# Mixture-of-experts trunk: the small experts' values turned in two pieces at other places of the gate-up, and up to three down blocks a step in the last pair of experts

## The chip, the cores and the metric

The kernel runs on one core of one Trainium2 chip. The metric is the device time of one execution in microseconds (us). TensorE is called PE in the profile, its weight loads PEld, VectorE DVE, ScalarE ACT, GpSimd POOL, SyncE SP; SP issues the weight loads by DMA.

## The reference, cut to what matters

The program is a decoder trunk of two layers over 256 tokens of 1024 channels, in fp32. The change touches the second layer's expert part alone, the last large stage before a gated embedding add and the final norm:

```python
def moe_swiglu(hn, w_router, w_gate_up, w_down):
    xt = hn.reshape(T, D)                       # 256 x 1024
    logits = (xt @ w_router).astype(jnp.float32)
    top_val, top_idx = lax.top_k(logits, TOP_K) # 2 of 8 experts
    gates = jax.nn.softmax(top_val, axis=-1)
    ...
    def expert_block(args):
        xb, e = args
        g, u = jnp.split(xb @ w_gate_up[e], 2, axis=-1)   # 1024 -> 2 x 3584
        return (jax.nn.silu(g) * u) @ w_down[e]           # 3584 -> 1024
    ...
    contrib = y[dest] * g_s[:, None].astype(y.dtype)
    out = jnp.zeros((T, D), y.dtype).at[tok_s].add(contrib)
```

All expert weights, 8 x (1024 x 7168 + 3584 x 1024) fp32 values, are read once.

## The kernel before

**Products in parts.** An fp32 matrix is split into two parts of the type fp32r: ACT casts the high part `h` (line 145), DVE subtracts it from the raw value and leaves the low part `l` (line 146). A raw weight tile is 1 MB (128 partitions x 2 x 1024); `wsplit` makes two halves of it, each with one cast and one subtraction. There are ten raw buffers and four buffers each for `h` and `l`. DMA fills a raw buffer as soon as its last reader has given it back.

**Two sizes of experts.** The experts are sorted by their number of tokens and taken in the order 0, 4, 1, 5, 2, 6, 3, 7. Experts 0 to 3 ("large") have 128 slots for tokens and need three products for each pair of tiles: h x h, l x h, h x l. Experts 4 to 7 ("small", `few(e)` in the code) have 64 slots; the high and low parts of their tokens stand side by side in the 128 columns, so two products do, and the two halves of the result have to be added.

**Steps.** The hidden width 3584 is cut in chunks of 1024, 1024, 1024 and 512 columns. One step makes the gate and up values of one chunk (`gate_up`): eight channel tiles k, in each 1 MB of gate and up weights; a large expert has 96 products of 512 columns there, a small one 64. 32 steps cover 8 experts; the step's chunk is `now`. Behind the gate-up the step multiplies "down" blocks (`back`, `down`) that belong to chunks finished earlier, usually of the expert before: a block is 512 hidden columns, 2 MB of weights (`r_d`, parts `h_d`, `l_d`), 24 products into `y` for a large expert, 16 for a small one. Before step 8 (RAMP) there is one block a step, from then on two. So a full step from step 8 on has 8 + 4 MB of weights and 16 + 8 halves. After the last down block of an expert, `combine` splits y (`yh`, `yl`, lines 197 and 198), multiplies by the slots (`cb`) and adds to `h` (DVE, line 1260).

**From values to the left operand of down.** A chunk's values must be transposed. For a large expert silu and product come first (`msg`), then `across` transposes a block on PE (`mt<-cst,msg`, line 1226), and `h_T` splits it (`mhh` on ACT, `mhl` on DVE). For a small expert the gate and up values are copied (`msg`, `msu`); in the next step `turn` multiplies each piece of 512 columns by `both`, a matrix that transposes and adds the two halves at once (`mt<-both,msg`, 16 instructions of 64 columns a piece), then `turned` applies silu (ACT, line 1215) and the product (DVE, line 1216) to give `mgu`, and `h_T` splits it (`mh`).

**What sets the order.** A scheduler orders the instructions of each engine by the place at which the code issues them, and moves one ahead where it is ready; `after(...)` pins an instruction behind a named earlier one. Each engine then runs its instructions in order. `gate_up` calls a hook ahead of certain channel tiles; the four hooks of a step, at the tiles of MIDS = (1, 3, 4, 6), counted from 0, are: `turn_fresh` (all pieces of the last chunk), `fresh_turned`, `blocks_across`, `blocks_split`. `turn` has no pin, `turned` and `blocks_split` stand behind the last split issued so far. The hooks run when the split of their tile has been issued.

**The end.** The last pair is experts 3 and 7. Steps 28, 29 and 30 make 7's full chunks with two blocks of expert 3 each, step 31 makes 7's last chunk with the last block of 3. Then come 7's own blocks, two a step, and last the block (7, 3), loaded by halves of the columns (`r_dl`, `l_dl`), each half combined and normed at once.

Of the kernel before, what the change touches and what calls it, by code (L numbers as in the profile page):

```python
# [11 lines left out]
AF = mybir.ActivationFunctionType  # L12
ALU = mybir.AluOpType
AX = mybir.AxisListType
MUL, ADD, SUB, MAX = ALU.mult, ALU.add, ALU.subtract, ALU.max

P = 128
# [66 lines left out]
def trunk_kernel(  # L84
# [6 lines left out]
    pe, act, dve, pool, sync = nc.tensor, nc.scalar, nc.vector, nc.gpsimd, nc.sync  # L91
# [8 lines left out]
    def pa(name, shape=(P, 512)):  # L100
        return ps.tile(list(shape), F32, tag="a", name=name, bufs=4)

    def s2(name, shape, dt=F32):
        return ar.tile(list(shape), dt, tag="s2", name=name, bufs=S2_BUFS)
# [4 lines left out]
    def pt(name, shape=(P, 512)):  # L109
        return ps.tile(list(shape), F32, tag="t", name=name, bufs=2)  # L110
# [62 lines left out]
    def mm(o, a, b, start, stop, shared=False):  # L173
        last["mm"] = pe.matmul(o, a, b, start=start, stop=stop, skip_group_check=shared)  # L174
# [28 lines left out]
    def sub2(pr, *idx):  # L203
        return pr[0][idx], pr[1][idx]
# [17 lines left out]
    BLOCKS = [(b, n) for b in range(NB) for n in range(2)]  # L222
# [21 lines left out]
    def transpose_h(gname, k):  # L244

        q = (pt, py)[k // 4](f"nt_{gname}_{k}", (P, 2, T))
        for b in range(NB):
            for j in range(2):
                pe.transpose(q[:, j, b * P : (b + 1) * P], h[:, b, (k + j) * P : (k + j + 1) * P], ident)
        return q  # L250
# [112 lines left out]
    def ple_proj(i, pT, mark=""):  # L363


        raw = wraw(tview(ple_w_proj[i], 0, 2 * P, 0, D), (2, D), f"pj{i}{mark}")
        if i == 0:
            wt = wsplit(raw, f"pj{i}{mark}")
            wt = {(k, n): sub2(wt[k], slice(None), HALF[n]) for k in range(2) for n in range(2)}
        else:  # L370

            wt = {}
            for k in range(2):
                for n in range(2):
                    wt[k, n] = (s2(f"pwh{i}{k}{n}{mark}", [P, 512], F32R), s2(f"pwl{i}{k}{n}{mark}", [P, 512], F32R))
                    with (ExitStack() if mark else after("yh", "yl")):
                        split(wt[k, n], raw[:, k, HALF[n]])
        banks, res = {}, [[None, None] for b in range(NB)]

        def product(b, n, bank=pa):  # L380
            q = banks[b, n] = bank(f"pj{i}_{b}{n}{mark}")
            for k in range(2):
                mm3(q, sub2(pT, slice(None), k, slice(b * P, b * P + P)), wt[k, n], k == 0, k == 1)

        def copy(b, n):
            res[b][n] = s2(f"pj{i}{b}{n}{mark}", [P, 512])
            act.copy(res[b][n], banks[b, n])

        return product, copy, res
# [553 lines left out]
    def layer1_moe(pT):  # L943
# [3 lines left out]
        product, copy, pj1 = ple_proj(1, pT)  # L947
# [7 lines left out]
        for k in range(0, KT, 2):  # L955
            q = transpose_h("ffn1", k)
# [97 lines left out]
        def few(e):  # L1054
            return e >= FEW
# [115 lines left out]
        def gate_up(e, c, at):  # L1171

            ns = CHUNKS[c][1] // 512
            banks = [[pa(f"m{nm}{e}{c}{i}") for i in range(ns)] for nm in "gu"]
            for k, j, wt in gate_up_weights(e, c):
                if j == 0 and k in at:
                    at[k]()
                products(e, [(banks[j][i], tokens[e][k], sub2(wt, slice(None), slice(i * 512, i * 512 + 512))) for i in range(ns)],
                         k == 0, k == KT - 1)

            def activate():

                res = []
                with after("wcopy", "wsplit"):
                    for i in range(ns):
                        if few(e):
                            res.append([s2(f"ms{nm}{e}{c}{i}", [P, 512]) for nm in "gu"])
                            for j in range(2):
                                act.copy(res[i][j], banks[j][i])
                            continue  # L1190
                        sg = s2(f"msg{e}{c}{i}", [P, 512])
                        act.activation(sg, banks[0][i], AF.Silu)
                        dve.tensor_tensor(sg, banks[1][i], sg, MUL)
                        res.append(sg)
                return res

            return activate

        def turn(e, c):


            res = []
            for i, sg in enumerate(hidden[e, c]):
                q = pt(f"mt{e}{c}{i}", (P, 2, 4, P // 2))
                for j in range(2):
                    for g in range(2):
                        for k in range(2):
                            mm(q[:, j, 2 * g + k, :], sg[j][:, 256 * g + k : 256 * g + 256 : 2], both, True, True)
                res.append(q)
            return res  # L1210

        def turned(e, c, banks):
            t = s2(f"mgu{e}{c}", [P, len(banks), 4, P // 2])
            for i, q in enumerate(banks):
                act.activation(t[:, i], q[:, 0], AF.Silu)
                dve.tensor_tensor(t[:, i], q[:, 1], t[:, i], MUL)
            hidden[e, c] = t

        def across(e, c, i):

# [41 lines left out]
        yb, hT, hidden = {}, {}, {}  # L1262
        both = sm("both", (P, P // 2))
# [87 lines left out]

        gates_up = [(e, c) for e in ORDER for c in range(len(CHUNKS))]
        downs = [(e, c, n) for e in ORDER for c in range(len(CHUNKS)) for n in range(CHUNKS[c][1] // 512)]
        stored = dr.tile([P, NB, 2, 512], F32, name="pj1d")
        fresh = None
        while gates_up or len(downs) > 1:
            now = gates_up.pop(0) if gates_up else None
            step = NE * len(CHUNKS) - len(gates_up) - 1 if now else None
            n = next((i for i, d in enumerate(downs) if d[:2] not in hidden), len(downs))
            n = min(1 if now and step < RAMP else 2, n, sum(d[0] == downs[0][0] for d in downs))  # L1360
            blocks, downs = downs[:n], downs[n:]
            if step == QUAD:
                spread_slots = gather(2)
            if step == SLOTS:
                spread_slots()
            if step == PAIR:
                gather(1)
            banks = {}

            def turn_fresh():  # L1370
                if fresh and few(fresh[0]):
                    banks["fresh"] = turn(*fresh)
                if now == (0, LATE):
                    for bn in todo:
                        product(*bn, pt)
                        copy(*bn)
                    for b, i in BLOCKS:
                        act.dma_start(stored[:, b, i], pj1[b][i])

            def fresh_turned():  # L1380
                if "fresh" in banks:
                    with after("wcopy", "wsplit"):
                        turned(*fresh, banks["fresh"])

            def blocks_across():
                for d in blocks:
                    banks[d] = across(*d)

            def blocks_split():
                with after("wcopy", "wsplit"):  # L1390
                    for d in blocks:
                        hT[d] = h_T(*d, banks[d])

            if now:
                activate = gate_up(*now, dict(zip(MIDS, (turn_fresh, fresh_turned, blocks_across, blocks_split))))

                def between(now=now, activate=activate):
                    hidden[now] = activate()
            else:
                for f in (turn_fresh, fresh_turned, blocks_across, blocks_split):  # L1400
                    f()
                between = None
            for i, d in enumerate(blocks):
                back(*d, between if len(blocks) == 1 else None)
                if i == 0 and len(blocks) == 2 and between:
                    between()
            if not blocks:
                between()
            if step == 0:
                with after("wsplit"):  # L1410
                    gates()
            fresh = now
        if fresh:
            turned(*fresh, turn(*fresh))
        last_norm = halves_norm_T("ple1")
        for b, i in BLOCKS:
            pj1[b][i] = s2(f"pj1{b}{i}", [P, 512])
# [24 lines left out]
    pj1, norm1, overflow = layer1_moe(pT1)  # L1442
# [50 lines left out]
    with tc.If(over):  # L1493
        more()
        product, copy, pj1 = ple_proj(1, ple_T(1, pt, "v"), "v")
# [7 lines left out]
RAW_BUFS = 10  # L1503
PAD = 8
CONV_DVE = (31, 31, 5, 9)
MIDS = (1, 3, 4, 6)
RAMP = 8
ORDER = (0, 4, 1, 5, 2, 6, 3, 7)
FEW = 4
QUAD, SLOTS, PAIR = 3, 8, 13  # L1510
# [2 lines left out]
LATE = 1  # L1513
# [36 lines left out]
```

## Time and profile before

| | |
|---|---|
| median of 3 runs | 1492.35 us (1490.93 to 1492.8) |
| profiled execution | 1491.29 us, its span 1489.5 us |
| mean granted clock of PE | 0.992 |
| busy: PE, DVE, ACT | 1436.0, 1263.3, 1067.8 us |
| experts, from the first gate-up to the last combine | 528 to 1451 us of the span |
| DMA | 440.36 MB, mean 296 GB/s |

A row of the timeline has start and length in us, the engine, the line, and output <- inputs by their names in the program (numbers left out); a bracket behind it is the idle time ahead of it and what ended it. PE's matmuls are pipelined, so their shown lengths overlap, and a product's price is read from start to start or from the chain.

### The profile page before, as it was taken

What the parts mean: (1) busy time and instruction counts of PE and PEld (TensorE: products, weight loads), DVE (VectorE), ACT (ScalarE), POOL (GpSimd) and SP (SyncE); (2) the same over time, 40 slices, a digit from 0 to 9 for tenths busy, and PEclk for the clock granted to TensorE, in tenths of its full rate; (3) what the DMA queues carried; (4) which work ended last, traced back from release to release, by engine and by line L of the source; (5) the groups of instructions that cost most, each with busy time, mean ns of one, the idle gap of its engine ahead of it and who ended that gap; (6) DMA issues with size and microseconds to landing.
All of it is one profiled execution on the core that took longest, in us unless ns stands there. A gap on an engine that the chain in (4) does not pass through costs nothing.

```text
span 1489.5 us, 22041 instructions
## 1 busy us (share of the span) xinstructions
PE 1436.0 (96%) x7726; PEld 1202.4 (81%) x7726; DVE 1263.3 (85%) x1716; ACT 1067.8 (72%) x1441; POOL 4.9 (0%) x14
## 2 busy tenths in 40 slices
PE   7999999999999999999999999999999999999996
PEld 6999899988897878877877677877677877677755
DVE  6778655546698699999999989899999899999887
ACT  6545544446557677888888888788888788888675
POOL 0000000000000000000000000000000000000000
PEclk9999999999999999999999999999999999999999
DMA  9514655555452469999999999999999999999960
GB/s 350 215 39 133 212 184 187 182 195 179 152 203 95 140 228 388 342 404 405 366 396 407 384 345 381 356 400 408 400 386 396 354 398 408 400 395 385 360 237 31
DMA packets 137762, 440.36 MB, mean 296 GB/s; under 512 B 9195, under 2 KB 34316, under 8 KB 123564
## 3 DMA queue, kind: packets, MB, share of 16 engines
q1 hardware_dynamic: 133536, 434.24, 77.7%
q10 hardware_dynamic: 3724, 3.36, 0.7%
q0 software_dynamic: 384, 1.29, 0.3%
q8 instruction: 62, 1.02, 0.3%
q14 instruction: 56, 0.46, 0.1%
HBM read 435.97 MB, written 2.88 MB: 295 GB/s over the span
## 4 chain that ended last, share of the span: by engine, by line
PE 74%; DVE 14%; issue 4%; ACT 4%; DMA 2%; ACTq 0%; DVEq 0%; POOL 0%; POOLq 0%
PE y L174 14%; PE mg L174 13%; PE mu L174 13%; DVE l L146 6%; PE fu L174 4%; PE fg L174 4%; PE fd L174 4%; PE mt L174 3%; PE wo L174 3%; PE pg L174 3%; DVE l_d L146 2%; PE p L174 1%; DMA r_gu<-in_moe_w_gate_up_dram 1%; ACT h L145 1%; PE in_og L174 1%
## 5 line engine op out<-in xcount | busy, mean ns | idle before, releaser
L146 DVE TENSOR_TENSOR l<-r_gu,h 128x1024 fp32r<-128x1024 f32 x448 | 524.8, 1218 | 33.2 <-ACT h L145 25.7
L145 ACT CAST h<-r_gu 128x1024 fp32r<-128x1024 f32 x448 | 458.1, 1053 | 93.0 <-PE y L174 34.8
L146 DVE TENSOR_TENSOR l_d<-r_d,h_d 128x1024 fp32r<-128x1024 f32 x220 | 257.2, 1218 | 9.4 <-ACT h_d L145 5.7
L145 ACT CAST h_d<-r_d 128x1024 fp32r<-128x1024 f32 x220 | 221.8, 1056 | 24.1 <-PE mu L174 7.8
L146 DVE TENSOR_TENSOR l_gu<-r_gu,h_gu 128x1024 fp32r<-128x1024 f32 x44 | 53.8, 1224 | 47.6 <-ACT h_gu L145 47.6
L145 ACT CAST h_gu<-r_gu 128x1024 fp32r<-128x1024 f32 x44 | 46.0, 1048 | 64.2 <-PE fu L174 49.0
L174 PE MATMUL y<-l_d,mh 128*128 128x512 f32 x216 | 73.8, 423 | 3.6 <-DVE l_d L146 3.6
L174 PE MATMUL y<-l_d,mhh 128*128 128x512 f32 x224 | 70.8, 397 | 0.0
L174 PE MATMUL y<-h_d,mhh 128*128 128x512 f32 x224 | 70.3, 395 | 0.0
L174 PE MATMUL y<-h_d,mh 128*128 128x512 f32 x216 | 68.5, 399 | 1.3 <-DVE mh L198 1.3
L174 PE MATMUL y<-h_d,mhl 128*128 128x512 f32 x224 | 69.3, 390 | 0.0
L174 PEld LDWEIGHTS y<-l_d,mh 128*128 128x128 f32 x216 | 37.0, 191 | 29.2 <-DVE l_d L146 24.7
L146 DVE TENSOR_TENSOR l_fd<-r_fd,h_fd 128x1024 fp32r<-128x1024 f32 x22 | 26.9, 1225 | 27.3 <-ACT h_fd L145 26.3
L174 PE MATMUL fg<-x_ffn0h,h_gu 128*128 128x256 f32 x176 | 49.9, 283 | 0.0
L174 PE MATMUL fu<-x_ffn0h,h_gu 128*128 128x256 f32 x176 | 49.9, 283 | 0.0
L174 PE MATMUL fg<-x_ffn0h,l_gu 128*128 128x256 f32 x176 | 49.9, 283 | 0.0
L174 PE MATMUL fu<-x_ffn0l,h_gu 128*128 128x256 f32 x176 | 49.8, 283 | 0.0
L174 PE MATMUL fu<-x_ffn0h,l_gu 128*128 128x256 f32 x176 | 49.8, 283 | 0.0
L174 PE MATMUL fg<-x_ffn0l,h_gu 128*128 128x256 f32 x176 | 49.8, 283 | 0.0
L174 PEld LDWEIGHTS y<-h_d,mh 128*128 128x128 f32 x216 | 41.2, 191 | 10.6 <-DVE mh L198 1.5
L174 PEld LDWEIGHTS y<-h_d,mhl 128*128 128x128 f32 x224 | 42.0, 188 | 9.2
L174 PEld LDWEIGHTS y<-l_d,mhh 128*128 128x128 f32 x224 | 40.8, 188 | 9.4 <-DVE l_d L146 1.8
(719 smaller groups left out, 3671.5 us busy)
## 6 DMA issues: line engine op xcount, KB each, us to landing
r_gu<-in_moe_w_gate_up_dram SPq DMA_DIRECT2D x192, 1024.0 KB, 7.9
r_d<-in_moe_w_down_dram SPq DMA_DIRECT2D x110, 1024.0 KB, 7.8
r_gu<-in_moe_w_gate_up_dram SPq DMA_DIRECT2D x64, 512.0 KB, 7.4
r_gu<-in_ffn_w_gate_up_dram SPq DMA_DIRECT2D x44, 512.0 KB, 4.9
r_fd<-in_ffn_w_down_dram SPq DMA_DIRECT2D x11, 1024.0 KB, 4.9
r_wo<-in_ev_w_out_dram SPq DMA_DIRECT2D x4, 1024.0 KB, 7.5
r_pg<-in_ple_w_gate_dram SPq DMA_DIRECT2D x4, 1024.0 KB, 5.5
r_wo<-in_od_w_out_dram SPq DMA_DIRECT2D x4, 1024.0 KB, 6.2
```

Of the source, the lines that this page charges most:

```text
L145: last["wcopy"] = act.copy(wh, raw[:, i : i + step])
L146: last["wsplit"] = dve.tensor_tensor(wl, raw[:, i : i + step], wh.bitcast(F32), SUB)
L174: last["mm"] = pe.matmul(o, a, b, start=start, stop=stop, skip_group_check=shared)
```

## The change

Two things. The turn of a small expert's values is issued a piece at a time, each pinned behind the last product issued so far: piece 0 ahead of tile 1, piece 1 ahead of tile 3; silu and product of a piece two tiles after its turn, the transposes of the large blocks at tile 5 as well, and the splits of the blocks at tile 7. And from step 28 (FAST) on a step with a chunk takes up to three down blocks, never the last one of all.

```diff
@@ -1196,25 +1196,26 @@
 
             return activate
 
-        def turn(e, c):
-
-
-            res = []
-            for i, sg in enumerate(hidden[e, c]):
-                q = pt(f"mt{e}{c}{i}", (P, 2, 4, P // 2))
+        def turn(e, c, i):
+
+
+            q = pt(f"mt{e}{c}{i}", (P, 2, 4, P // 2))
+            with after("mm"):
                 for j in range(2):
                     for g in range(2):
                         for k in range(2):
-                            mm(q[:, j, 2 * g + k, :], sg[j][:, 256 * g + k : 256 * g + 256 : 2], both, True, True)
-                res.append(q)
-            return res
-
-        def turned(e, c, banks):
-            t = s2(f"mgu{e}{c}", [P, len(banks), 4, P // 2])
-            for i, q in enumerate(banks):
-                act.activation(t[:, i], q[:, 0], AF.Silu)
-                dve.tensor_tensor(t[:, i], q[:, 1], t[:, i], MUL)
-            hidden[e, c] = t
+                            mm(q[:, j, 2 * g + k, :], raw_hidden[e, c][i][j][:, 256 * g + k : 256 * g + 256 : 2], both, True, True)
+            return q
+
+        raw_hidden = {}
+
+        def turned(e, c, i, q):
+            n = len(raw_hidden[e, c])
+            if i == 0:
+                hidden[e, c] = s2(f"mgu{e}{c}", [P, n, 4, P // 2])
+            t = hidden[e, c]
+            act.activation(t[:, i], q[:, 0], AF.Silu)
+            dve.tensor_tensor(t[:, i], q[:, 1], t[:, i], MUL)
 
         def across(e, c, i):
 
@@ -1357,7 +1358,7 @@
             now = gates_up.pop(0) if gates_up else None
             step = NE * len(CHUNKS) - len(gates_up) - 1 if now else None
             n = next((i for i, d in enumerate(downs) if d[:2] not in hidden), len(downs))
-            n = min(1 if now and step < RAMP else 2, n, sum(d[0] == downs[0][0] for d in downs))
+            n = min(1 if now and step < RAMP else 3 if now and step >= FAST else 2, n, sum(d[0] == downs[0][0] for d in downs), len(downs) - 1)
             blocks, downs = downs[:n], downs[n:]
             if step == QUAD:
                 spread_slots = gather(2)
@@ -1367,20 +1368,20 @@
                 gather(1)
             banks = {}
 
-            def turn_fresh():
-                if fresh and few(fresh[0]):
-                    banks["fresh"] = turn(*fresh)
-                if now == (0, LATE):
+            def turn_fresh(i):
+                if fresh and few(fresh[0]) and i < len(raw_hidden[fresh]):
+                    banks["fresh", i] = turn(*fresh, i)
+                if now == (0, LATE) and i == 0:
                     for bn in todo:
                         product(*bn, pt)
                         copy(*bn)
-                    for b, i in BLOCKS:
-                        act.dma_start(stored[:, b, i], pj1[b][i])
-
-            def fresh_turned():
-                if "fresh" in banks:
+                    for b, n in BLOCKS:
+                        act.dma_start(stored[:, b, n], pj1[b][n])
+
+            def fresh_turned(i):
+                if ("fresh", i) in banks:
                     with after("wcopy", "wsplit"):
-                        turned(*fresh, banks["fresh"])
+                        turned(*fresh, i, banks["fresh", i])
 
             def blocks_across():
                 for d in blocks:
@@ -1391,18 +1392,22 @@
                     for d in blocks:
                         hT[d] = h_T(*d, banks[d])
 
+            jobs = {1: [(turn_fresh, 0)], 3: [(fresh_turned, 0), (turn_fresh, 1)], 5: [(fresh_turned, 1), (blocks_across,)], 7: [(blocks_split,)]}
+            at = {k: (lambda fs=fs: [f[0](*f[1:]) for f in fs]) for k, fs in jobs.items()}
             if now:
-                activate = gate_up(*now, dict(zip(MIDS, (turn_fresh, fresh_turned, blocks_across, blocks_split))))
+                activate = gate_up(*now, at)
 
                 def between(now=now, activate=activate):
                     hidden[now] = activate()
+                    if few(now[0]):
+                        raw_hidden[now] = hidden[now]
             else:
-                for f in (turn_fresh, fresh_turned, blocks_across, blocks_split):
-                    f()
+                for k in sorted(at):
+                    at[k]()
                 between = None
             for i, d in enumerate(blocks):
                 back(*d, between if len(blocks) == 1 else None)
-                if i == 0 and len(blocks) == 2 and between:
+                if i == 0 and len(blocks) > 1 and between:
                     between()
             if not blocks:
                 between()
@@ -1411,7 +1416,8 @@
                     gates()
             fresh = now
         if fresh:
-            turned(*fresh, turn(*fresh))
+            for i in range(len(raw_hidden[fresh])):
+                turned(*fresh, i, turn(*fresh, i))
         last_norm = halves_norm_T("ple1")
         for b, i in BLOCKS:
             pj1[b][i] = s2(f"pj1{b}{i}", [P, 512])
@@ -1503,8 +1509,8 @@
 RAW_BUFS = 10
 PAD = 8
 CONV_DVE = (31, 31, 5, 9)
-MIDS = (1, 3, 4, 6)
 RAMP = 8
+FAST = 28
 ORDER = (0, 4, 1, 5, 2, 6, 3, 7)
 FEW = 4
 QUAD, SLOTS, PAIR = 3, 8, 13
```

The tile numbers in the following rows are those of one build each, and differ between the two.

On PE, in step 22 (the third chunk of expert 6), before: the y products of expert 2, and among them the turn of expert 6's second chunk (`mt610`, `mt611`).

```order
L174 MATMUL y20_10582<-l_d2_1_1_1_10898,mhh210_10835 128x512
L174 MATMUL y21_10583<-l_d2_1_1_1_10898,mhh210_10835 128x512
L174 MATMUL mt610_10997<-both_5572,msg610_10913 128x64 x4
L174 MATMUL mt610_10997<-both_5572,msu610_10914 128x64 x3
L174 MATMUL y20_10582<-h_d2_1_2_0_10923,mhh211_10839 128x512
L174 MATMUL y21_10583<-h_d2_1_2_0_10923,mhh211_10839 128x512
L174 MATMUL y20_10582<-h_d2_1_2_0_10923,mhl211_10840 128x512
L174 MATMUL y21_10583<-h_d2_1_2_0_10923,mhl211_10840 128x512
L174 MATMUL mt610_10997<-both_5572,msu610_10914 128x64
L174 MATMUL mt611_11006<-both_5572,msg611_10917 128x64 x2
L174 MATMUL y20_10582<-l_d2_1_2_0_10924,mhh211_10839 128x512
L174 MATMUL y21_10583<-l_d2_1_2_0_10924,mhh211_10839 128x512
```

The same place after: the turn stands behind the products of channel tile 0 (`h_6_2_0`, `l_6_2_0`), its second piece behind those of tile 2.

```order
L174 MATMUL mu620_10967<-l_6_2_0_1_10976,xe2h_6273 128x512
L174 MATMUL mu621_10968<-l_6_2_0_1_10976,xe2h_6273 128x512
L174 MATMUL mt610_10997<-both_5572,msg610_10913 128x64 x4
L174 MATMUL mt610_10997<-both_5572,msu610_10914 128x64 x4
L174 MATMUL mg620_10965<-h_6_2_1_0_10989,xe2h_6273 128x512
L174 MATMUL mg621_10966<-h_6_2_1_0_10989,xe2h_6273 128x512
...
L174 MATMUL mu621_10968<-l_6_2_2_1_11021,xe2h_6273 128x512
L174 MATMUL mt611_11045<-both_5572,msg611_10917 128x64 x4
L174 MATMUL mt611_11045<-both_5572,msu611_10918 128x64 x4
L174 MATMUL mg620_10965<-h_6_2_3_0_11034,xe2h_6273 128x512
```

No turn is left between y products; piece 0 stands between tiles 0 and 1, piece 1 between tiles 2 and 3.

On DVE, at the end of step 22's gate-up, before: the splits `mhl` of the two blocks of expert 2 stand around the first half of tile 7.

```order
L146 TENSOR_TENSOR l_6_2_6_1_11117<-r_gu6_2_6_11110,h_6_2_6_1_11116 128x1024
L198 TENSOR_TENSOR mhl220_11121<-mt220_11074,mhh220_11120 128x512
L146 TENSOR_TENSOR l_6_2_7_0_11139<-r_gu6_2_7_11136,h_6_2_7_0_11138 128x1024
L198 TENSOR_TENSOR mhl221_11125<-mt221_11079,mhh221_11124 128x512
L146 TENSOR_TENSOR l_6_2_7_1_11143<-r_gu6_2_7_11136,h_6_2_7_1_11142 128x1024
L146 TENSOR_TENSOR l_d2_2_0_0_11157<-r_d2_2_0_11154,h_d2_2_0_0_11156 128x1024
L146 TENSOR_TENSOR l_d2_2_0_1_11161<-r_d2_2_0_11154,h_d2_2_0_1_11160 128x1024
```

After, at the same place:

```order
L146 TENSOR_TENSOR l_6_2_6_1_11117<-r_gu6_2_6_11110,h_6_2_6_1_11116 128x1024
L146 TENSOR_TENSOR l_6_2_7_0_11131<-r_gu6_2_7_11128,h_6_2_7_0_11130 128x1024
L146 TENSOR_TENSOR l_6_2_7_1_11135<-r_gu6_2_7_11128,h_6_2_7_1_11134 128x1024
L198 TENSOR_TENSOR mhl220_11139<-mt220_11092,mhh220_11138 128x512
L146 TENSOR_TENSOR l_d2_2_0_0_11157<-r_d2_2_0_11154,h_d2_2_0_0_11156 128x1024
L198 TENSOR_TENSOR mhl221_11143<-mt221_11097,mhh221_11142 128x512
L146 TENSOR_TENSOR l_d2_2_0_1_11161<-r_d2_2_0_11154,h_d2_2_0_1_11160 128x1024
```

Both splits moved behind the second half of tile 7; the second now has the first `l_d` ahead of it.

On PE, at the end of expert 3, before: the last y products of expert 3, the products of its combine (`cb`), the turn of expert 7's last chunk and the first y product of expert 7.

```order
L174 MATMUL y31_12585<-l_d3_3_1_1_13395,mhh330_13350 128x512
L174 MATMUL cb300_13414<-yh30_13410,ohT10_8676 128x512
L174 MATMUL cb301_13418<-yh30_13410,ohT10_8676 128x512
L174 MATMUL cb300_13414<-yl30_13411,ohT10_8676 128x512
L174 MATMUL cb301_13418<-yl30_13411,ohT10_8676 128x512
L174 MATMUL cb310_13426<-yh31_13422,ohT10_8676 128x512
L174 MATMUL cb311_13430<-yh31_13422,ohT10_8676 128x512
L174 MATMUL cb310_13426<-yl31_13423,ohT10_8676 128x512
L174 MATMUL cb311_13430<-yl31_13423,ohT10_8676 128x512
L174 MATMUL mt730_13434<-both_5572,msg730_13384 128x64 x4
L174 MATMUL mt730_13434<-both_5572,msu730_13385 128x64 x4
L174 MATMUL y70_13452<-h_d7_0_0_0_13456,mh700_13446 128x512
```

After, the combine of expert 3 stands in the gate-up of expert 7's last chunk:

```order
L174 MATMUL mu730_13330<-h_7_3_0_0_13334,xe2h_6273 128x512
L174 MATMUL cb300_13309<-yh30_13305,ohT10_8676 128x512
L174 MATMUL cb301_13313<-yh30_13305,ohT10_8676 128x512
L174 MATMUL mg730_13329<-l_7_3_0_0_13335,xe2h_6273 128x512
L174 MATMUL mu730_13330<-l_7_3_0_0_13335,xe2h_6273 128x512
L174 MATMUL mg730_13329<-h_7_3_0_1_13338,xe2h_6273 128x512
L174 MATMUL mu730_13330<-h_7_3_0_1_13338,xe2h_6273 128x512
L174 MATMUL mg730_13329<-l_7_3_0_1_13339,xe2h_6273 128x512
L174 MATMUL mu730_13330<-l_7_3_0_1_13339,xe2h_6273 128x512
L174 MATMUL cb300_13309<-yl30_13306,ohT10_8676 128x512
L174 MATMUL cb301_13313<-yl30_13306,ohT10_8676 128x512
L174 MATMUL mg730_13329<-h_7_3_2_0_13362,xe2h_6273 128x512
```

Products of the gate-up (`mg730`, `mu730`) stand between those of the combine, the turn of the third chunk follows (not shown), and the last chunk is turned behind the y products of (7, 1, 0).

## Rows read from the trace of the kernel before

**Rows 1.** The page: busy us of two engines; the costliest group.

```profile
PE 1436.0 (96%) x7726; PEld 1202.4 (81%) x7726; DVE 1263.3 (85%) x1716; ACT 1067.8 (72%) x1441; POOL 4.9 (0%) x14
...
L146 DVE TENSOR_TENSOR l<-r_gu,h 128x1024 fp32r<-128x1024 f32 x448 | 524.8, 1218 | 33.2 <-ACT h L145 25.7
```

**Rows 2.** Waits, 600 to 1489 us: us in total, times, longest us.

```profile
ACT h L145 <- PE y L174: 34.0, 42, 2.0
PEld mu L174 <- DVE l L146: 26.7, 45, 1.0
...
ACT mgu L1215 <- PE mt L174: 13.7, 7, 6.4
```

**Rows 3.** Waits of the loads' own queue (SyncE), the same stretch.

```profile
SPq L766 <- DVE l L146: 185.9, 99, 4.1
```

**Rows 4.** Windows by step: PE, PEld, DVE, ACT, POOL busy, PEclk, DMA share, GB/s.

```profile
676.10:702.20 26.10, 25.30 (x125) 20.17 (x124) 24.04 (x24) 22.22 (x28) 0.00 (x0) 1.00 1.03 404
865.50:902.10 36.60, 35.07 (x192) 29.11 (x191) 32.85 (x37) 29.37 (x40) 0.00 (x0) 1.00 0.92 336
...
1062.10:1095.90 33.80, 31.22 (x134) 22.00 (x134) 32.52 (x33) 27.85 (x32) 0.00 (x0) 1.00 1.00 386
...
1128.20:1160.40 32.20, 31.11 (x154) 25.48 (x153) 29.65 (x29) 27.04 (x32) 0.00 (x0) 1.00 1.02 391
1160.40:1177.80 17.40, 17.40 (x84) 14.37 (x83) 15.40 (x16) 13.90 (x17) 0.00 (x0) 1.00 0.99 381
1212.50:1242.70 30.20, 30.00 (x129) 23.71 (x128) 29.55 (x30) 25.94 (x29) 0.00 (x0) 1.00 1.02 413
...
1405.40:1421.40 16.00, 11.53 (x36) 8.44 (x36) 10.34 (x14) 6.83 (x10) 0.00 (x0) 0.68 0.76 267
```

**Rows 5.** The chain in order of time, 1311 to 1346 us: start, us, what.

```profile
1312.69 5.47 PE y L174 x24
1318.17 1.59 PE mt L174 x14
...
1326.46 0.65 PE mt L174 x6
```

**Rows 6.** DVE timeline, 1317 to 1358 us: start, us, line, [idle before <-releaser].

```profile
1333.12 0.75 DVE L1216 TENSOR_TENSOR mgu<-mt,mgu 128x256 f32<-128x256 f32 x2
...
1342.32 0.68 DVE L198 TENSOR_TENSOR mhl<-mt,mhh 128x512 fp32r<-128x512 f32 x1
...
1344.06 9.16 DVE L146 TENSOR_TENSOR l_d<-r_d,h_d 128x1024 fp32r<-128x1024 f32 x8
1354.26 1.23 DVE L146 TENSOR_TENSOR l<-r_gu,h 128x1024 fp32r<-128x1024 f32 x1 [1.04 <-ACT h L145]
```

**Rows 7.** PE timeline, 872 to 886 us (step 13): transposes L1226.

```profile
883.08 1.11 PE L1226 MATMUL mt<-cst,msg 128*128 128x128 f32 x8
883.94 0.70 PE L174 MATMUL mg<-l,xe2l 128*128 128x512 f32 x2
```

**Rows 8.** The chain, 660 to 695 us (step 5 into 6).

```profile
679.97 0.88 PE mt L174 x8
```

**Rows 9.** DVE timeline, 876 to 886 us (step 13).

```profile
882.48 0.42 DVE L1216 TENSOR_TENSOR mgu<-mt,mgu 128x256 f32<-128x256 f32 x1 [1.46 <-ACT mgu L1215]
```

**Rows 10.** PE timeline, 1385 to 1450 us, the end of expert 3.

```profile
1404.83 0.61 PE L174 MATMUL y<-l_d,mhh 128*128 128x512 f32 x2
```

**Rows 11.** DVE timeline, 1400 to 1451 us.

```profile
1405.87 0.69 DVE L198 TENSOR_TENSOR yl<-y,yh 128x512 fp32r<-128x512 f32 x1 [0.77 <-ACT yh L197]
...
1407.96 1.40 DVE L1260 SCALAR_TENSOR_TENSOR h<-cb,Gr,h 128x512 f32<-128x512 f32 x2
...
1415.94 0.42 DVE L1216 TENSOR_TENSOR mgu<-mt,mgu 128x256 f32<-128x256 f32 x1 [2.39 <-ACT mgu L1215]
...
1424.77 0.75 DVE L198 TENSOR_TENSOR mh<-mgu,mh 128x256 fp32r<-128x256 f32 x2
...
1444.62 3.48 DVE L146 TENSOR_TENSOR l_dl<-r_dl,h_dl 128x1024 fp32r<-128x1024 f32 x3
```

## Prediction

> **What bounds the kernel now.** I read the page first, for busy time: PE is busy 1436.0 of 1489.5 us and DVE 1263.3, and the costliest group is the subtraction `l`, 448 times 1218 ns [rows 1]. Neither engine's share says where time is lost, so next the waits of the expert stretch: ACT's casts wait for the down products, PE waits for `l`, and a `mgu` silu waits once for 6.4 us for its turn [rows 2]. That is a ring: the casts wait for PE to free the part buffers, PE waits for the parts. Then the loads' own queue: its longest wait is for DVE's `l`, that is for a raw buffer to be given back, 185.9 us in 99 waits [rows 3]. So the loads are held back, and no transfer sets the pace. Then one window a step [rows 4]: a full step of a large expert is 30.20 us with DVE 29.55 busy; a full step of a small one is 32.20 with DVE 29.65 and PE 31.11. Equal DVE work, 2 us more. The chain through such a step [rows 5] shows why: behind the gate-up's end the 48 down products run as pieces of y (24 in 5.47 us: 0.228 each), and between them stand the turns (`mt`, 14 passes 1.59 us; 32 passes cost 3.54). While PE turns it frees no part buffer, so ACT stands still, and then DVE: it is idle 1.04 us at the first `l` of the next gate-up [rows 6]. Afterwards, in the gate-up, DVE is the bound and PE waits. The step pays PE's turn in the one half and DVE's excess in the other.
>
> **The change, part by part.** Prices: a 512-column product 0.228, a turned piece 1.77 (half of 3.54) [rows 5]; a DVE half 1.14 (eight in 9.16), a `mgu` 0.38 (two in 0.75), an `mhl` 0.65 between its neighbours [rows 6]; transposes 0.43 a block (two blocks start to next 0.86) [rows 7].
>
> *Turns into the gate-up.* No instruction is added. In a full small step the two halves become: gate-up, PE 64 x 0.228 + 3.54 + 0.86 = 18.99, DVE 16 x 1.14 + 0.75 = 18.99; down, PE 48 x 0.228 = 10.94, DVE 8 x 1.14 + 2 x 0.65 = 10.42, since the two `mhl` move from the gate-up to behind the last `l` of tile 8. PE's sum is 29.9, DVE's 29.65 as now. Both halves are balanced, so neither engine can reach its floor exactly; the large step stands 0.65 above its DVE time [rows 4], and I take the same: 29.9 + 0.65 = 30.6, 1.6 less than 32.20. From both sides: 30.0 (no allowance, gain 2.2) and 31.4 (half of the present excess stays, gain 0.8). It holds for three steps outside the last pair (expert 5's third, expert 6's second and third): **4.8**, ends 2.4 and 6.6. With one down block (steps 5 and 6) the row is 26.10 with DVE 24.04 [rows 4], PE's floor 14.59 + 3.54 + 0.43 + 5.47 = 24.0, so 1.4 at most; but there half of the turn stands between gate-up products already (8 passes at 679.97, 8 more behind) [rows 8], so I take half, 0.75 each: **1.5**, ends 0 and 2.8. Step 13 has its turns in the gate-up now and is 36.60 long for other work: 0. The short fourth steps (17.40 long, PE busy 17.40 [rows 4]) are bound by PE in all: 0. Large steps that turn the one last piece have the same sum on PE: 0.
>
> *The splits behind the eighth tile.* In the first step of a small expert (33.80 long, DVE 32.52, PE 31.22 [rows 4]) nothing is turned; DVE is the bound of its gate-up, and the two `mhl` leave it for the down half, where DVE has slack: up to 1.3, I take half, 0.7 for steps 12 and 20: **1.4**, ends 0 and 2.6. What they hold up there: `l_d` stands behind each, so the first is 0.65 later. PE covers it with the last two gate-up products (0.46) and four y products from `h_d` (0.91). The second split belongs to the second block, 5.47 later.
>
> *Three blocks.* No work is added; the last pair's 14 down blocks go earlier. Now the end has a hole: from 1405.4 to 1421.4 DVE is busy 10.34 of 16.00 and PE 11.53, at a granted clock of 0.68 [rows 4]: combine of expert 3, the turn of the last chunk and the first y of expert 7 follow one another with no gate-up left to fill in. After it DVE runs almost without a gap until the third `l_dl` ends at 1444.62 + 3.48 = 1448.10 [rows 11]. The new course:
> Step 28: y started at 1312.69 [rows 5]; 1.3 of `mhl` leaves DVE's gate-up, a third transpose adds 0.43: 1311.8. Then 72 products, 16.4, and 0.5 for `l_d` behind the splits: 1328.7.
> Step 29: 14.59 + 3.54 + 3 x 0.43 + 16.4 + 0.65 = 36.5: 1365.2.
> Step 30, one block: 14.59 + 3.54 + 0.43 + 5.47 + 0.65 = 24.7: expert 3's last product ends at 1389.9, where it now ends at 1404.83 + 0.61 = 1405.44 [rows 10].
> From there DVE is the bound. It has, behind the second `l` of the last gate-up (1.1 later), 33 halves to the third `l_dl` (6 of the gate-up, 24 of six blocks, 3 `l_dl`): 37.6; two `yl` of 0.65 and four `h` of 0.67: 4.0; three `mgu` of 0.38 and seven `mh` of 0.36: 3.7 [rows 11]. PE has less, about 41 (112 y and 32 gate-up products, 3 pieces, 8 `cb`). The waits that I leave: the last turn stands behind the y of (7,1,0), and of DVE only two `l_d` (2.3) stand ahead of its `mgu`, against 0.7 + 1.77 + 0.4 on PE and ACT, then an `h_d`: 1.3 together. So 1389.9 + 1.1 + 45.3 + 1.3 = 1437.6, **10.5** earlier; what follows is as it was. The loads move with their blocks on SP's queue; ahead of the gate-up of (7,1) stand six `r_d` where there were four. Ends: 5 (the hole's idle time comes back elsewhere) and 13.
>
> Sum: 4.8 + 1.5 + 1.4 + 10.5 = 18.2; the ends added are 7.4 and 25. The profiled execution took 1491.29 us for its span of 1489.5, and is 1.06 under the median, 1492.35. So 1491.29 - 18.2 + 1.06 = **1474.2**.
>
> **Rivals.** *A: the hole moves instead of closing.* For: the 6.4 us wait of `mgu` [rows 2] comes of a turn with nothing behind it, and (7,3) is still turned after the last gate-up; combine (`yh`, `cb`, `h`) still needs two PSUM tiles in turn. Against: eight halves of gate-up now lie around the combine. If the idle 16.00 - 10.34 = 5.66 stays, 1474.2 + 5.7 = 1479.9.
>
> *B: the loads become the bound.* A full step moves 12 MB, 12.58 million bytes, and in 30.6 us needs 411 GB/s; small steps now get 391, the large ones 413 with the same bytes [rows 4]. For: 413 is the highest row, and no margin shows. Against: [rows 3], the queue waits for DVE. If 391 were all, the three steps stay (4.8 lost) and step 29 with 14 MB takes 37.5 (1.1 lost): 1480.1. The Trainium skill has a rule against the change here: "DMA: Bandwidth & Descriptors", Specifications, puts a NeuronCore's limit at about 358 GB/s. By it 12.58 MB take 35.1 us, and no full step could be under that; this trace's 413 and 391 disagree, so it gets no chance beyond that of B.
>
> *C, slower: the silus wait for their turns.* ACT and DVE run in order, and a `mgu` ahead of its turn stops all casts behind it. In step 13, the one step with its turns wholly in the gate-up, DVE stands 1.46 us before the second `mgu` [rows 9] and 0.24 before the first. If every other piece (six of each small expert less step 13's two, 22) costs 1.70, that is 37: 1474.2 + 37 = 1511. It ends slower from 0.83 a piece on. Against: piece 0 is turned ahead of tile 2's products, and its silu stands behind the casts of tile 4, which need the buffers that tile 2's products free; so the turn is done when ACT gets there. In step 13 the turn stood later. Only the short steps lack this cover.
>
> *D: no change.* `mhl` and `mh` now stand directly ahead of y. If PE waits for both in every full step from step 8 on, nine small ones by 1.3 and nine large ones by 0.72, 18.2 takes back the sum: 1492.4. Against: the cover above (1.37), and that the second is not needed yet.
>
> **The numbers.** The forecast gets 0.60 (own range 1468 to 1479), A 0.15, B 0.10, C 0.08, D 0.07. A measurement of this kernel tells about 0.2%, 3 us, from no change. Faster: forecast, A and B, 0.85; same: D, 0.07; slower: C, 0.08. The range runs from 1467 (all upper ends together, 25) to 1484, which takes in A and B with their own error and leaves out C and D.
>
> **What would show it.** In the windows, expert 6's second and third step at 30.0 to 31.4 with DVE's idle time under 1.5 us; in the chain, no `mt` between y products. Around the combine of expert 3 the gate-up's products, a granted clock of 1.00, and the third `l_dl` near 1437 to 1438. It is wrong if `mgu` waits for `mt` or ACT grow (C), if ACT's casts wait for DMA (B), if PE's first y products wait for `mhl` or `l_d` by more than 0.5 (D), or if DVE's idle time behind the last turn is above 3 us (A).

## The result, and the profile after

The changed kernel takes 1473.36 us (median of 4, 1471.79 to 1473.94) against 1491.76 (median of 4, 1490.93 to 1492.8); the ratio is 0.9875, 95% interval 0.9858 to 0.9892. The forecast was 1474.2.

The page of the changed kernel, the row that answers to the first of [rows 1]:

```profile
PE 1429.4 (97%) x7726; PEld 1201.4 (82%) x7726; DVE 1261.1 (86%) x1716; ACT 1066.9 (72%) x1441; POOL 4.9 (0%) x14
```

The instructions are the same in number and DVE's busy time to 2.2 us, so what DVE lost is idle time. Of PE's 17.3 us of span 6.6 had been shown as busy (1436.0 to 1429.4), and 10.7 were idle. The windows of the changed kernel, one step each, in the columns of [rows 4]: step 6, 13, 20, 22 and 23, a full large step (25), and the 16 us behind expert 3's last product.

```profile
677.00:701.80 24.80, 24.73 (x126) 20.49 (x125) 24.12 (x24) 22.22 (x28) 0.00 (x0) 1.00 1.03 403
864.70:899.30 34.60, 34.07 (x180) 28.36 (x179) 32.79 (x37) 30.05 (x42) 0.00 (x0) 1.00 0.94 349
1057.90:1090.70 32.80, 31.03 (x123) 21.06 (x122) 32.47 (x33) 28.97 (x33) 0.00 (x0) 1.00 1.00 390
1121.20:1151.70 30.50, 30.50 (x153) 25.65 (x153) 29.29 (x29) 26.79 (x33) 0.00 (x0) 1.00 1.03 406
1151.70:1169.70 18.00, 18.00 (x98) 15.55 (x97) 15.32 (x16) 13.26 (x17) 0.00 (x0) 1.00 1.02 407
1204.20:1234.40 30.20, 30.00 (x129) 23.71 (x128) 29.55 (x30) 25.93 (x29) 0.00 (x0) 1.00 1.02 413
1381.20:1397.20 16.00, 15.51 (x80) 12.04 (x78) 15.39 (x21) 11.39 (x17) 0.00 (x0) 1.00 0.88 349
```

Beside [rows 4]: the full small step went from 32.20 to 30.50, and PE has no idle time left in it; step 13 from 36.60 to 34.60, step 20 from 33.80 to 32.80, step 6 from 26.10 to 24.80; the large step is the same to the hundredth. The short step is longer, 18.00 for 17.40. In the last window DVE is busy 15.39 of 16.00, where the hole had 10.34, at a granted clock of 1.00 for 0.68.

The chain through step 22 of the changed kernel, 1120 to 1153 us; [rows 5] shows such a step of the kernel before:

```profile
1124.83 0.46 PE mu L174 x2
1125.28 1.82 PE mt L174 x16
1127.11 0.52 PE mg L174 x2
...
1130.82 1.82 PE mt L174 x16
...
1142.83 10.26 PE y L174 x44
```

From the first gate-up product to the last y everything on the chain is PE's: the pieces stand in one run each between gate-up products, and the 44 y products follow without a turn among them.

The waits of the changed kernel from 600 us on, beside [rows 2]:

```profile
ACT h L145 <- PE mg L174: 35.2, 61, 1.7
PEld y L174 <- DVE l_d L146: 34.3, 76, 1.2
ACT mgu L1217 <- PE mt L174: 18.9, 10, 3.7
...
PEld mu L174 <- DVE l L146: 14.6, 30, 0.8
...
ACT h L145 <- PE y L174: 8.8, 26, 1.5
```

The casts' waits for the y products fell from 34.0 to 8.8, and the waits of `mu`'s weight loads for `l` from 26.7 to 14.6. The casts now wait for gate-up products instead, 21 of the 35.2 us directly behind a turned piece. In step 22 that wait is off the path, since the chain above is PE's alone. The waits of `mgu` for its turn grew, from 13.7 in 7 waits to 18.9 in 10; what they cost is looked at below.

The DVE timeline at the end of the changed kernel:

```profile
1388.22 2.35 DVE L146 TENSOR_TENSOR l<-r_gu,h 128x1024 fp32r<-128x1024 f32 x2
...
1396.70 15.98 DVE L146 TENSOR_TENSOR l_d<-r_d,h_d 128x1024 fp32r<-128x1024 f32 x14
1413.47 0.42 DVE L1218 TENSOR_TENSOR mgu<-mt,mgu 128x256 f32<-128x256 f32 x1 [0.79 <-ACT mgu L1217]
1413.81 0.75 DVE L198 TENSOR_TENSOR mh<-mgu,mh 128x256 fp32r<-128x256 f32 x2
1415.02 6.90 DVE L146 TENSOR_TENSOR l_d<-r_d,h_d 128x1024 fp32r<-128x1024 f32 x6 [0.45 <-ACT h_d L145]
...
1427.05 3.49 DVE L146 TENSOR_TENSOR l_dl<-r_dl,h_dl 128x1024 fp32r<-128x1024 f32 x3
```

The last turn costs 0.79 + 0.45 of DVE; the third `l_dl` ends at 1430.54, 17.56 earlier than in [rows 11].

### The profile page after: what moved, and what is told of

Its sections match the earlier page's. It is cut to its first block, busy times and chain, and to the rows that moved or that the text cites. A ratio compares the mean times of both kernels' runs of the same rounds, so it can differ in the third digit from the quotient of the medians.

```text
span 1472.2 us, 22039 instructions
## 1 busy us (share of the span) xinstructions
PE 1429.4 (97%) x7726; PEld 1201.4 (82%) x7726; DVE 1261.1 (86%) x1716; ACT 1066.9 (72%) x1441; POOL 4.9 (0%) x14
## 4 chain that ended last, share of the span: by engine, by line
PE 78%; DVE 12%; ACT 4%; issue 3%; DMA 2%; ACTq 0%; SPq 0%; DVEq 0%; POOL 0%; POOLq 0%
PE mg L174 15%; PE mu L174 15%; PE y L174 13%; PE fu L174 4%; PE fg L174 4%; PE fd L174 4%; DVE l L146 4%; PE mt L174 3%; PE wo L174 3%; PE pg L174 3%; DVE l_d L146 3%; PE p L174 1%; PE xg L174 1%; PE pj L174 1%; PE in_og L174 1%
## 5 line engine op out<-in xcount | busy, mean ns | idle before, releaser
L174 PEld LDWEIGHTS y<-l_d,mh 128*128 128x128 f32 x216 | 35.9, 188 | 30.5 <-DVE l_d L146 26.6
L174 PEld LDWEIGHTS y<-h_d,mhh 128*128 128x128 f32 x224 | 41.8, 188 | 9.1 <-ACT h_d L145 0.3
## 6 DMA issues: line engine op xcount, KB each, us to landing
r_pg<-in_ple_w_gate_dram SPq DMA_DIRECT2D x4, 1024.0 KB, 10.7
```

## The experiments

Eleven kernels. Each ratio is to runs of the kernel before on the same chip; its medians there were 1491.4 to 1492.1. "Changed kernel" is the one above, at 1473.36; differences from it are between medians whose runs need not be of one chip, and the intervals are about 2.5 us to either side, so less than that is read from the traces or not at all. The full small step named is step 22.

**turns_only.** `FAST = 28` becomes `FAST = 99`.

> The changed kernel with two down blocks a step to the end, so only the moved turns, silus, transposes and splits. My theory (the turn pays while PE is bound by y, and costs nothing in the gate-up where DVE is the bound): all full small steps keep their 1.7 us, those of the last pair too, and the hole at the end of expert 3 stays with DVE idle some 5 us: 1479 to 1480. Rival (the gain is that of the last pair's blocks alone): 1486 or more. Rival (both parts needed together): 1490.

1478.01 (ratio 0.9907, 0.9890 to 0.9924). The windows of this kernel, step 22 and the 16 us behind expert 3's last product:

```profile
1120.30:1150.80 30.50, 30.50 (x154) 25.68 (x152) 29.28 (x30) 26.82 (x33) 0.00 (x0) 1.00 1.03 406
1391.50:1407.50 16.00, 12.12 (x39) 8.53 (x38) 10.30 (x15) 7.39 (x11) 0.00 (x0) 0.68 0.79 277
```

That is 1 us under the range of my theory. The steps keep all they won, and the hole is there as in [rows 4], DVE idle 5.70. So the blocks are worth 4.6; in the traces the last pair, from step 28's start to the third `l_dl`, takes 155.2 here and 150.7 in the changed kernel, 4.5 less.

**three_blocks_only.** The kernel before, with the new count of blocks:

```diff
-n = min(1 if now and step < RAMP else 2, n, sum(d[0] == downs[0][0] for d in downs))
+n = min(1 if now and step < RAMP else 3 if now and step >= FAST else 2, n, sum(d[0] == downs[0][0] for d in downs), len(downs) - 1)
-if i == 0 and len(blocks) == 2 and between:
+if i == 0 and len(blocks) > 1 and between:
```

> The kernel before with up to three down blocks a step from step 28 on, the hooks at tiles 1, 3, 4 and 6 as before. My theory: the hole at the end closes, the full small steps stay at 32.2 us with the turns among the y products: 5 to 7 us faster than before, 1485 to 1487. Rival (the last pair owes its 9 us to the blocks): 1482. Rival (both parts needed together): within 0.2% of before.

1487.21 (0.9969, 0.9956 to 0.9981), 4.9 faster than before at 1492.1. The 16 us behind expert 3's last product in this kernel:

```profile
1394.90:1410.90 16.00, 15.34 (x76) 11.11 (x75) 14.25 (x18) 11.71 (x17) 0.00 (x0) 1.00 0.77 290
```

The hole closes, at a granted clock of 1.00 for 0.68. Step 22 is 32.2 us as before. The two parts add up: 14.1 and 4.9, against 18.4 together, which the scatter of the runs allows.

**turn_not_pinned.** `with after("mm"):` around the turn's products becomes `with ExitStack():`.

> The changed kernel without the pin of the turn behind the last product, so that the scheduler moves the first piece and part of the second back among the y products; the silus stay two tiles later, the splits at tile 8, three blocks in the last pair. My theory: what counts is where the turn stands on PE, so a full small step goes back towards 32 us (most of the turn is in y again): 1479 to 1484. Rival (the silus and splits that stand later are what pays): 1473 to 1475.

1477.42 (0.9900, 0.9883 to 0.9916), 4.1 slower than the changed kernel and still under the range of my theory. The scheduler puts piece 0 and part of piece 1 back among the y products, and step 22 takes 31.8 us with DVE idle 2.1. Less is lost than the whole 1.7 a step: the later silus and splits keep 0.4, and the short steps are 0.6 shorter than in the changed kernel, since their turn is done before they start.

**silu_at_once.**

```diff
-jobs = {1: [(turn_fresh, 0)], 3: [(fresh_turned, 0), (turn_fresh, 1)], 5: [(fresh_turned, 1), (blocks_across,)], 7: [(blocks_split,)]}
+jobs = {1: [(turn_fresh, 0), (fresh_turned, 0)], 3: [(turn_fresh, 1), (fresh_turned, 1)], 5: [(blocks_across,)], 7: [(blocks_split,)]}
```

> The changed kernel with the silu and product of each piece issued at the same tile as its turn, not two tiles later, so that nothing covers the wait for the turn. The forecast's rival C at its price of 1.7 us a piece for 22 to 24 pieces: 37 to 41 us slower than the changed kernel, 1510 to 1514. My theory (DVE has some 1.2 us of slack a step, and PE some parts ahead): 0.4 to 1.2 a piece, 1483 to 1500. If the cover never mattered: 1473 to 1475.

1496.04 (1.0026, 1.0016 to 1.0036): slower than the kernel before. The waits of this kernel from 600 us on:

```profile
ACT mgu L1217 <- PE mt L174: 64.1, 28, 3.7
...
DVE mgu L1218 <- ACT mgu L1217: 29.6, 26, 1.9
```

Without the two tiles of cover ACT waits for each of the 28 pieces, and step 22 takes 33.0 us, 1.25 more a piece. Over all 28 it is 22.7 us, 0.81 each: under the 1.70 that the forecast took for 22 pieces, and enough to eat the whole gain. Rival C was a real mechanism, and the two tiles are what keeps it out.

**splits_at_six.** In `jobs`, `7: [(blocks_split,)]` becomes `6: [(blocks_split,)]`.

> The changed kernel with the splits of the down blocks issued at tile 6 as before, not at tile 7: two mhl stand around the first half of tile 7 again. My theory (DVE is the bound of the gate-up in steps 12, 20 and 28, so 1.3 us of mhl there is paid): those three steps lose 0.5 to 1.1 each, the other full small steps have PE as their bound and lose 0 to 0.7: 1475 to 1479. Rival D of the forecast (the splits in front of y hold PE up): as fast or faster than the changed kernel, 1470 to 1473.5.

1477.12 (0.9903, 0.9886 to 0.9919), 3.8 slower than the changed kernel. The time lies in the range of my theory, but not where it put the loss. Step 22 is 30.9 long and step 21 31.2, for 30.5; step 14 loses 0.6, steps 5 and 6 0.5 each, step 12 0.4. Step 20 stays at 32.8 and step 28 is 0.4 shorter, though PE is idle 2.5 in step 20 where the changed kernel has 1.8. So most of what the splits are worth lies in the steps that turn; my reading, not tested apart, is that DVE's gate-up pays for them there too. Rival D, by which the splits in front of y hold PE up, falls: with the splits moved away from y the kernel is slower.

**three_blocks_once.** `FAST = 28` becomes `FAST = 30`.

> The changed kernel with FAST = 30: expert 3's blocks go 2, 2, 3 in steps 28 to 30 instead of 3, 3, 1. My theory (what pays is only that expert 3's last block lies before the last gate-up, so that its combine has work around it): the same time as the changed kernel, 1472 to 1475. Rival (the gain is from loads and blocks that start earlier in step 28): half of the 4.6 us is lost, 1475.5 to 1478.

1472.49 (0.9876, 0.9859 to 0.9892), not to be told from the changed kernel. Steps 28 and 29 are 32.8 and 30.5 long with two blocks, step 30 takes 36.6 with three: what pays is where expert 3 ends, not how its blocks are spread.

**eight_raw_buffers.** `RAW_BUFS = 10` becomes `RAW_BUFS = 8`.

> The changed kernel with 8 raw buffers of 1 MB instead of 10. My theory (the loads wait for DVE to give buffers back, and have margin): within 0.3% of the changed kernel, 1472 to 1477, full small steps still 30.5. Forecast's rival B (at 406 to 415 GB/s the loads are all but the bound): a step loses more than 1 us, 1485 or more.

1471.84 (0.9866, 0.9850 to 0.9882). Step 22 of this kernel:

```profile
1120.40:1150.90 30.50, 30.50 (x154) 25.68 (x153) 29.26 (x29) 26.81 (x33) 0.00 (x0) 1.00 1.03 405
```

2 MB less of loads ahead cost nothing at 405 GB/s: the loads need no more lead than 8 buffers give, and the last pair takes 150.7 as well. That alone does not say that the rate is no limit; for that see the last experiment.

**short_step_silus_later.** For chunks of 512 columns alone:

```diff
+if now and CHUNKS[now[1]][1] < 1024:
+    jobs = {1: [(turn_fresh, 0)], 3: [(turn_fresh, 1)], 5: [(fresh_turned, 0), (blocks_across,)], 7: [(fresh_turned, 1), (blocks_split,)]}
```

> The changed kernel with the silus of the short steps (512 columns) two tiles later, at tiles 5 and 7, where ACT no longer waits 2.1 and 1.5 us for the turn. If DVE's 2.65 us of idle time in these steps is on the path (the steps grew from 17.4 to 18.0): about 0.6 us in each of three steps and more in the last, 1470 to 1472. If PE is the bound there (it shows no idle time): no change that can be told, 1472.5 to 1474.5.

1474.37 (0.9882, 0.9866 to 0.9899). The waits of `mgu` for `mt` in the three short steps are gone, yet these steps became longer, by 0.7 to 0.8 each (18.7 instead of 18.0 for step 23), and the step behind each is only 0.2 shorter: no gain. So the waits were not on the path; PE has no idle time in a short step of the changed kernel. Why the steps grew was not followed up.

**turned_whole_at_one.** In `jobs`, `(turn_fresh, 1)` moves from tile 3 to tile 1.

> The changed kernel with both pieces turned together behind tile 0, 3.5 us of PE in one run, the silus still at tiles 3 and 5. If two pieces matter (PE frees no part buffer for 3.5 us, DVE has four halves ahead at most and then stands): 0.5 to 1.5 a full small step, 1476 to 1484. If only the place in the gate-up matters: 1472 to 1475.

1481.34 (0.9929, 0.9911 to 0.9945), 8.0 slower than the changed kernel. The waits in step 22 of this kernel:

```profile
ACT h L145 <- PE mg L174: 3.5, 1, 3.5
DVE l L146 <- ACT h L145: 2.5, 1, 2.5
```

ACT has one wait of 3.5 us, the whole turn, and passes 2.5 on to DVE; the step is 31.7 long. DVE has 1.2 us to spare in this step, so 1.2 to 1.3 of the 2.5 come through. In this kernel the four part buffers cover 1.8 us of PE that frees none, not 3.6. So the cut in two pieces is worth 1.2 of this step's 1.7.

**turn_one_tile_later.** In `jobs`, the keys 1, 3, 5 become 2, 4, 6.

> The changed kernel with turns and silus one tile later: turns at tiles 2 and 4, silus at 4 and 6, transposes at 6. My theory (PE's sum is the bound of a full small step, wherever in the gate-up the turn stands): 1472 to 1476. If the place is tuned to a tile: 1478 or more.

1474.74 (0.9888, 0.9871 to 0.9904). Step 22 is 30.2 long, others are longer (step 21 30.7, the short steps 17.8 to 18.3, the large step behind them up to 34.9 for 34.4); the place is not tuned to a tile.

**first_piece_turned_twice.** Piece 0 is turned twice, the second time to the same values:

```diff
-for j in range(2):
+for j in range(2) if i else (0, 1, 0, 1):
```

> The changed kernel with piece 0 of every small chunk turned twice, the same values: 16 more instructions runs of 1.8 us on PE, nothing on DVE. My theory (PE is the bound of the full small steps and of the short ones now): all of it is paid in 14 to 16 of 16 places, 25 to 29 us slower than the changed kernel, 1498 to 1502. If DVE were still the bound there (its slack of 1.2 us a step would hide most): 1478 to 1485.

1501.58 (1.0068, 1.0051 to 1.0085), 28.2 slower than the changed kernel: 16 pieces of 1.77 are 28.3, at the 1.82 of the chain 29.1. Step 22 of this kernel:

```profile
1135.00:1167.40 32.40, 32.40 (x169) 27.58 (x169) 29.32 (x30) 26.84 (x33) 0.00 (x0) 1.00 1.00 378
```

1.9 us of PE make the step 1.9 longer. PE is the bound there now, and every us of it is paid. This also settles rival B: if the loads had set the pace, the added work would have been hidden behind them, and here their rate only falls, from 406 to 378 GB/s.

## Why the prediction was right, point by point

The lengths are from the first `l` of one step to that of the next in the DVE timelines, before and after.

| term | forecast | measured |
|---|---|---|
| three full small steps | 4.8 | 5.2 (1.7 each) |
| steps 5 and 6 | 1.5 | 2.5 (1.1 and 1.4) |
| steps 12 and 20 | 1.4 | 1.5 (0.4 and 1.1) |
| step 13 | 0 | 2.0 |
| short steps 7, 15, 23 | 0 | -1.6 (0.3 and twice 0.6 longer) |
| large steps 8, 16, 24 | 0 | 0.8 |
| last pair, from step 28's start to the third `l_dl` | 10.5 | 9.3 (160.0 to 150.7) |
| sum | 18.2 | 19.7 |

The profile shows 17.56 at the third `l_dl`: the other 2.1 us were lost ahead of the change's first step, 0.5 of them before the first `l` of the experts and 1.6 in the first expert step (last section), which is the same program in both. That the medians differ by 18.4, within 0.2 of the forecast, is therefore partly luck: terms that came out 4.3 above the forecast in all and 2.8 below it cancel in part, and in the profile the time lost ahead of the change hides the remaining 1.5.

*Full steps.* The mechanism stood as forecast, and the size to 0.1. One part of it was off: the 0.65 taken from the large step was called an allowance for two balanced engines. The chain shows no such imbalance; the step is PE's own sum, with the pieces at 1.82, the y products at 0.233 (44 in 10.26) and the gate-up products at 0.231 instead of 1.77 and 0.228. DVE has 1.2 us to spare. So the allowance had the right size for another reason, which was luck.

*Step 13* was put at 0 "for other work", although [rows 7] and [rows 9] were read. Two things were overlooked. The first is its 1.70 us of DVE idle time before the two `mgu`, which served as the price of rival C and not as something that the change would take away. Both pieces still stand in one run there (32 passes), but the second silu now comes two tiles later. The DVE timeline of the changed kernel in step 13:

```profile
879.82 0.42 DVE L1218 TENSOR_TENSOR mgu<-mt,mgu 128x256 f32<-128x256 f32 x1 [0.23 <-ACT mgu L1217]
...
884.17 0.42 DVE L1218 TENSOR_TENSOR mgu<-mt,mgu 128x256 f32<-128x256 f32 x1
```

With the silus put back (silu_at_once) the step takes 35.55 for 34.61, 0.9 of the 2.0 back. The second is where the turn stood. In the kernel before, 20 of the 32 passes that belong to step 14's turn stood among the y products of step 13. Without the pin (turn_not_pinned) they return there, and step 13 takes 35.26, 0.65 more. The y products shown for step 22 under "The change" are of the same kind: those before belong to the blocks (2, 1), that is to the down half of step 21.

*Step 20* is the same case, and most of its 1.1 was booked to the wrong cause. It has no turn of its own, but in the kernel before 20 passes of step 21's turn stood among its y products, here in the chain of the kernel before:

```profile
1092.11 1.59 PE mt L174 x14
...
1094.68 0.65 PE mt L174 x6
```

The forecast gave it 0.7 for the splits. With the splits put back it stays at 32.8 (splits_at_six); with the turn put back by leaving out the pin it takes 33.4, which is 0.6 of the 1.1. The rest was not taken apart. In the changed kernel DVE is idle only 0.3 in the whole step, so it makes no difference there in which half the splits stand.

*Short steps* were put at 0 since PE is their bound in all. That is why they grew: the turn of the third chunk, which stood partly in the y products of the step ahead, is now wholly in theirs. Of the 1.7 of that step 0.6 comes back one step later, and turn_not_pinned has it at 17.4 again.

*The splits* had a term of their own for steps 12 and 20 alone. Taken back (splits_at_six) they cost 3.8: the whole 0.4 of step 12, nothing in step 20, 0.4 to 0.7 in each full small step, and 0.5 in each of steps 5 and 6, which is 1.1 of the 2.5 there that the forecast sought in the turns alone.

*Large steps* were put at 0 and won 0.3 each. None of the runs that take back the pin or the splits changes that, and its cause is open.

*The last pair* came out at 9.3 for 10.5, and its course was met closely: counted from step 28's start, 8.3 earlier than before, the third `l_dl` at 1438.8 for the forecast's 1437.6, with 1.24 of waits behind the last turn for 1.3. But the term stood under "three blocks", and the blocks are worth 4.6 to 4.9; the rest is the same gain of moved turns and splits in steps 28 to 30: in turns_only these three are 1.1, 1.8 and 1.7 shorter than before. Part of what the blocks won goes with PE's clock, to which the forecast gave no price of its own. Around the combine in the hole of the kernel before, PE waited 1.50 and 1.06 us; then came a stretch at a granted clock of 0.50, the lower of its two levels, with the last turn and the first y products on the chain. The window and the chain of the kernel before:

```profile
1411.80:1421.20 9.40, 8.13 (x27) 6.97 (x28) 4.47 (x7) 3.07 (x5) 0.00 (x0) 0.50 0.68 221
```

```profile
1411.81 3.69 PE mt L174 x16
...
1416.75 4.64 PE y L174 x10
```

In the changed kernel the same turn takes half as long (8 passes in 0.88), at a granted clock of 1.00 (PE timeline):

```profile
1411.03 1.04 PE L174 MATMUL mt<-both,msg 128*128 128x64 f32 x8
1411.91 1.11 PE L174 MATMUL mt<-both,msu 128*128 128x64 f32 x8
```

No run separates what the clock gave back from the waits that the blocks filled.

*The rivals.* A did not happen: DVE is idle 0.61 of 16.00 where it was 5.66. B did not happen: PE is busy all 30.50 us of the full step, and more of PE's work makes it longer (first_piece_turned_twice); with eight raw buffers it is as long, at 405 GB/s. The limit of about 358 GB/s in the Trainium skill's "DMA: Bandwidth & Descriptors", Specifications, does not hold for these loads on one core. C was held off by the two tiles. Its sign, longer waits of `mgu` for `mt`, did appear (13.7 to 18.9), but the ten waits lie in the short steps, in step 13 and in the last step, none in a full small step, and taking those of three short steps away won nothing (short_step_silus_later). D did not happen: the waits of y's weight loads for `l_d` grew from 26.4 to 34.3 us in all, but the full small steps show no idle time of PE, and splits_at_six, which takes the splits away from y, is slower.

## What to carry to other kernels

Where two engines feed each other through a few buffers, a step costs the sum of each half's bound: move work of the engine that is the bound of one half into the half where it waits, and look at both halves apart. Find out first in which step the work to be moved now stands: here 20 of 32 passes of a turn stood in the step ahead of the one that issued it, and the gain or the loss shows up there. Cut what is moved so that each piece is shorter than what the buffers cover (1.8 us passed, 3.6 did not), and put its consumer behind work that needs the same buffers to be freed, or the wait only changes engines. A hole at a hand-over between stages closes by letting the older stage end before the younger one's last independent work.

## What the runs showed of the hardware that was not expected

The first expert step, in which the gather products of the routing (`xg`) run, took one of two times in the thirteen profiles, although its program is the same in all: 37.1 to 37.2 us in nine, 38.8 in four. ACT waited 5.1 to 5.2 us in all for the gather products in the nine and 6.8 in the four. The waits in that stage, first before, then after:

```profile
ACT xe0h L200 <- PE xg L174: 5.2, 3, 4.3
```

```profile
ACT xe0h L200 <- PE xg L174: 6.8, 3, 5.9
```

The four are the changed kernel, splits_at_six, eight_raw_buffers and short_step_silus_later. No moved instruction explains the 1.6 us, which are near what the runs of one kernel differ by (1471.79 to 1473.94). But each kernel has one profile, so that the two times change between executions of one kernel is likely and not shown. The granted clock from 518 to 524 us was 0.82 before and 0.61 in the changed kernel, yet over all thirteen it does not part the groups: 0.72 to 0.91 in the nine, 0.61 to 0.76 in the four. What sets the time is left open.
